# Splitting a mixer's weights two units ahead of the products, in three pairs of buffers

## The chip, the cores and the metric

The kernel runs on one core of one Trainium2 chip. The metric is the device time of one execution in microseconds. The engines are named as in the profile: PE (TensorE matmuls), PEld (TensorE weight loads), DVE (VectorE), ACT (ScalarE), POOL (GpSimd) and SP (SyncE, which here issues nearly all transfers).

## The reference, cut to what matters

Two models run one after the other on 256 tokens of width 1024. The first block has two layers of attention and a convolutional feed-forward network. The second block puts 16 learned tokens in front (L = 272) and has two layers:

```python
for l in range(DEPTH):
    u = rms_norm(h, norm1_g[l])
    p = jnp.einsum("bld,dp->blp", u, w_in[l])
    p_a, p_b, p_c = _split(p, (A_TOTAL, B_TOTAL, C_TOTAL))
    y_a = rwkv7_group(p_a, ...)           # two scan directions, 4 heads
    y_b = diff_attention_group(p_b, ...)
    y_c = gla_group(p_c, ...)             # two scan directions
    h = h + jnp.einsum("blc,cd->bld", concat(y_a, y_b, y_c), w_out[l])
    h = h + expert_choice_ffn(rms_norm(h, norm2_g[l]), router[l], e_w1[l], e_w3[l], e_w2[l])
```

Everything up to the residual sum of `w_out` is called the mixer here; the change touches the two mixers alone. The experts (16 per layer, 1024 by 1408, three matrices each) follow every mixer.

## The kernel before, in words

**Split products.** Where a product needs more than the fast matmul format keeps, both operands are split into a rounded high part and a residual. `split` (L401, L403) makes the high part `whi` of a weight tile of 128 x 1024 with one ACT copy, and the residual `wlo` = weight - `whi` with one subtraction on DVE (on POOL for the 5th and 14th split of a mixer). A product then is three matmuls: high x high, high x residual of the activations, residual x high of the weights. So the third matmul of a unit is the first that needs `wlo`.

**Units.** A mixer has 28 units of projection (a weight tile of up to 128 columns against all 272 tokens: 8 x 3 matmuls) and 8 units of output projection. `units` is a generator: when the program asks for the next unit, it first loads and splits weights until `ahead` units beyond the one handed out are split. The pairs `whi`, `wlo` come from the pool `hl2` with `HL2` pairs; a split must wait until the last matmul that read its pair has ended. The raw weights are loaded by SP into a ring of three tiles (pool `wh`, L1327), and a slot is free when its split is done.

**Order.** PE's order is the program's order (a manual schedule). The program weaves generators: `first` and `second` are the recurrent heads (preparation, then the chains of small products, L1640 to L1824), two more do the other groups, and `others`, the units, fills in between them. The chains wait for named units. In a chain the products of AR and KB (of the first direction, two groups of ten, then of the second) come early; AR and KB are written by DVE at L1566 to L1569. The order on ACT, DVE, POOL and SP is made by the framework's scheduler from the program's order, the priorities and what each instruction waits for. Each of these queues runs in order.

**Memory.** A reserved scratch lies at the low end of each partition. Pools are stacked above it: what lives throughout, then for a mixer its results (`mt`), the ring of weights (`wh`), the normalized activations (`mxu`), the pairs (`hl2`), and above them small working pools, constants, the heads' tiles and the chains' tiles. From the high end hang the first chain's tiles, then the eight output weights, and after the mixer six of the experts' seven large weight buffers. The seventh and three smaller ones are stacked on `mt` from below. A load into an expert buffer waits until all tiles of the mixer that lay there are done with. Of the large ones the first two in use lie 32 to 64 KB below the high end, over the second chain's tiles; the next two lie below these.

The change names `SCR` (L246), `HL2` (L273) and the call of `units` in `project` (L1386 to L1388).

Of the kernel before, what the change touches and what calls it, by code (L numbers as in the profile page):

```python
# [242 lines left out]
EXTRAR = 6  # L243
EXTRAL = 3
EXTRAU = 0
SCR = 16384  # L246
TURN2 = 0
AH = 2
RW = 'tile'
# [20 lines left out]
EXTRA1 = 4  # L270
EXTRA2 = 7
HL1 = 3
HL2 = 2  # L273
TUNE = [{'pool': [5, 14], 'lat': [1.6, 1.846, 1.296, 1.183], 'late': [0, 0, 4.19, 0], 'share': [0.419, 0.319], 'order': [('s', 6), ('s', 7), ('s', 3), ('s', 5), ('s', 1), ('s', 2), ('s', 0), ('gq', 0), ('gk', 0), ('s', 4), ('s', 8), ('gad', 0), ('q', 0), ('q', 1), ('q', 2), ('k', 1), ('k', 2), ('k', 3), ('gv', 0), ('q', 3), ('k', 0), ('gv', 1), ('v', 0), ('v', 1), ('v', 2), ('v', 3), ('sg', 0), ('sg', 1)], 'prep': 2.18, 'last': 2, 'halves': 2.02, 'passes': [0, 2, 1, 3]}, {'pool': [5, 14], 'lat': [1.6, 1.846, 1.296, 1.183], 'late': [0, 0, 4.19, 0], 'share': [0.419, 0.319], 'order': [('s', 6), ('s', 7), ('s', 3), ('s', 5), ('s', 1), ('s', 2), ('s', 0), ('gq', 0), ('gk', 0), ('s', 4), ('s', 8), ('gad', 0), ('q', 0), ('q', 1), ('q', 2), ('k', 1), ('k', 2), ('k', 3), ('gv', 0), ('q', 3), ('k', 0), ('gv', 1), ('v', 0), ('v', 1), ('v', 2), ('v', 3), ('sg', 0), ('sg', 1)], 'prep': 2.18, 'last': 2, 'halves': 2.02, 'passes': [0, 2, 1, 3]}]

# [936 lines left out]
def second_block(K, tap, st=None):  # L1212
# [3 lines left out]
    with ExitStack() as c2x:  # L1216
# [95 lines left out]
        def mixer(l, mixT, swr, cm, ce, nst):  # L1312
# [5 lines left out]
            uT = [U.tile([128, KD, L], F32R, name=f"u{i}") for i in range(2)]  # L1318
            K.hl = cm.enter_context(tc.tile_pool(reuse_waits=RW, name="hl2", bufs=HL2))
            DF = cm.enter_context(tc.tile_pool(reuse_waits=RW, name="df", bufs=1))  # L1320
# [39 lines left out]
            def project(R, box):  # L1360
# [23 lines left out]
                for hp in range(2):  # L1384
                    shifted_to.update({hp: rT[:, hp, :L], 2 + hp: kT[:, hp, :L], 4 + hp: vT[:, hp, :L]})
                us = K.units([unit(JOBS.index(j)) for j in tune["order"]] +  # L1386
                             [lambda i=i, j=j: wouts[2 * i + j][:, None, :] for i in tune["passes"] for j in range(2)],
                             ahead=1)  # L1388

                def cds(name):  # L1390
                    o, n = CD[name]
# [691 lines left out]
            c1, c0 = ExitStack(), ExitStack()  # L2083
            R1 = c1.enter_context(tc.tile_pool(reuse_waits=RW, name="rw1", bufs=1, side="right"))
            prep, rest, us = project(c0.enter_context(tc.tile_pool(reuse_waits=RW, name="mxs", bufs=1)), box)

            def first():
# [376 lines left out]
```

## Time and profile before

| | |
|---|---|
| median of 3 runs | 2652.69 us |
| the three runs | 2651.7, 2652.69, 2666.6 us |
| the profiled execution | 2655.46 us, span 2653.7 us |
| mean granted TensorE clock | 0.948 |
| PE busy | 2462.8 us, 93% |
| PEld busy | 1509.8 us, 57% |
| DVE busy | 1084.4 us, 41% |
| ACT busy | 755.6 us, 28% |
| POOL busy | 207.0 us, 8% |
| read from HBM | 749.54 MB, 283 GB/s over the span |

The span is from the first to the last instruction of the program; an execution takes 1.8 us more. All numbers of a row of the trace belong to one execution, which was 2.8 us above the median. A granted clock of 1.00 is 2.4 GHz and 0.50 is 1.2 GHz; a mean between them is a share of time at either level. A busy share is a mean over stages: the mixers of the second block lie at 769 to 1057 and 1705 to 2003 us, its experts behind them.

### The profile page before, as it was taken

The numbers are of one execution on the slowest core, as the hardware profiler recorded it, in microseconds if no ns is written. First come the engines' busy times: TensorE is split into PE (matmuls) and PEld (weight loads), VectorE is DVE, ScalarE is ACT, GpSimd is POOL, SyncE is SP. The second block draws the span as 40 slices with busy tenths as digits, with TensorE's granted clock in tenths as the row PEclk, the third lists the DMA queues.
The fourth block names the chain that finished last, engine by engine and source line by source line (L and its number), as shares of the span: only waits on it lengthen the run. The fifth ranks groups of instructions, "written<-read, shape, count | busy, mean of one in ns | idle before, by whom it ended". The sixth has DMA issues, their size and how long they took to land. (4 is left out here: it accounts for less than half of the span.)

```text
span 2653.7 us, 43625 instructions
## 1 busy us (share of the span) xinstructions
PE 2462.8 (93%) x18599; PEld 1509.8 (57%) x18599; DVE 1084.4 (41%) x2308; ACT 755.6 (28%) x1471; POOL 207.0 (8%) x260
## 2 busy tenths in 40 slices
PE   6989999899989998999999989999999999899898
PEld 4769988679978876333323322478774333233232
DVE  3557765567668466121111111365563122112112
ACT  3545545545445242110100100253331101000001
POOL 0011011110023211000000000122110000000000
PEclk8999999999989898999999999878899999999999
DMA  9385443674132225999999999511249999999996
GB/s 368 143 367 226 175 168 127 252 307 181 40 109 68 89 89 237 369 426 426 424 426 425 425 425 425 222 59 58 105 168 373 424 426 424 424 426 424 426 425 256
DMA packets 78482, 753.43 MB, mean 284 GB/s; under 512 B 9632, under 2 KB 13616, under 8 KB 25040
## 3 DMA queue, kind: packets, MB, share of 16 engines
q1 hardware_dynamic: 75360, 748.38, 69.2%
q8 instruction: 146, 2.39, 0.4%
q10 hardware_dynamic: 2928, 2.26, 0.3%
q14 instruction: 48, 0.39, 0.0%
HBM read 749.54 MB, written 1.07 MB: 283 GB/s over the span
## 5 line engine op out<-in xcount | busy, mean ns | idle before, releaser
L388 PE MATMUL bank<-w,mixT 128*34 128x512 f32 (+1 forms) x3072 | 685.7, 580 | 77.7 <-DMA w<-in_ew 77.7
L388 PEld LDWEIGHTS bank<-w,mixT 128*34 128x34 f32 x3072 | 190.7, 115 | 539.6 <-issue 401.2
L403 DVE TENSOR_TENSOR wlo<-w,whi 128x1024 fp32r<-128x1024 f32 (+1 forms) x242 | 298.8, 1237 | 169.9 <-ACT whi L401 168.7
L401 ACT ACTIVATE whi<-w 128x1024 fp32r<-128x1024 f32 x246 | 258.2, 1053 | 317.8 <-PE bank L388 131.2
L388 PE MATMUL bank<-w,hT 128*34 128x512 f32 x1408 | 314.6, 594 | 0.0
L2322 ACT ACTIVATE hid<-bank 34x512 f32<-34x512 f32 (+1 forms) x96 | 53.3, 555 | 765.8 <-PE bank L388 765.8
L388 PE MATMUL up<-hF,whi 128*128 128x256 f32 x1408 | 256.5, 285 | 5.2 <-ACT hF L573 5.2
L388 PEld LDWEIGHTS up<-hF,whi 128*128 128x128 f32 x1408 | 219.4, 191 | 6.9 <-ACT hF L573 6.0
L2323 DVE COPY hid<-bank 34x512 f32<-34x512 f32 (+1 forms) x96 | 62.4, 650 | 382.7 <-ACT hid L2322 381.7
L2369 DVE TENSOR_TENSOR x<-x,bank 128x272 f32<-128x272 f32 x256 | 95.7, 433 | 298.1 <-PE bank L388 297.0
L388 PE MATMUL bank<-u,whi 128*128 128x272 f32 (+1 forms) x896 | 212.2, 330 | 2.5 <-ACT u L1293 2.3
L388 PE MATMUL up<-hF,wlo 128*128 128x256 f32 x704 | 199.2, 284 | 0.0
L388 PEld LDWEIGHTS bank<-w,hT 128*34 128x34 f32 x1408 | 77.8, 112 | 189.2 <-issue 187.3
L388 PEld LDWEIGHTS bank<-u,whi 128*128 128x128 f32 (+1 forms) x896 | 151.9, 204 | 20.4 <-issue 7.9
L388 PE MATMUL bank<-u,wlo 128*128 128x272 f32 (+1 forms) x448 | 138.2, 309 | 6.0 <-DVE wlo L403 5.5
L388 PEld LDWEIGHTS up<-hF,wlo 128*128 128x128 f32 x704 | 134.2, 191 | 0.2
L452 POOL TENSOR_TENSOR rr<-rv,ca 128x3 f32<-128x3 f32 (+4 forms) x28 | 32.7, 1170 | 970.6 <-DVE rv L450 966.2
L2360 DVE COPY ys<-bank 34x512 f32<-34x512 f32 x32 | 22.2, 695 | 196.7 <-ACT ys L2359 196.7
L388 PE MATMUL acc<-gh,wlo 128*128 128x256 f32 x352 | 99.1, 281 | 0.0
L388 PE MATMUL acc<-gh,whi 128*128 128x256 f32 x352 | 99.0, 281 | 0.0
L388 PE MATMUL acc<-gl,whi 128*128 128x256 f32 x352 | 99.0, 281 | 0.0
L388 PEld LDWEIGHTS bank<-u,wlo 128*128 128x128 f32 (+1 forms) x448 | 91.6, 204 | 8.1 <-DVE wlo L403 7.0
(501 smaller groups left out, 3409.3 us busy)
## 6 DMA issues: line engine op xcount, KB each, us to landing
w<-in_ew SPq DMA_DIRECT2D x136, 2048.0 KB, 28.3
w<-in_ew SPq DMA_DIRECT2D x94, 1536.0 KB, 27.1
w<-in_ew SPq DMA_DIRECT2D x112, 1024.0 KB, 28.6
w<-in_ada SPq DMA_DIRECT2D x24, 2048.0 KB, 8.3
w<-in_ffn_up SPq DMA_DIRECT2D x22, 2048.0 KB, 8.4
w<-in_w_in SPq DMA_DIRECT2D x54, 512.0 KB, 3.4
w<-in_ffn_down SPq DMA_DIRECT2D x10, 2048.0 KB, 8.3
w<-in_ab_in SPq DMA_DIRECT2D x5, 2048.0 KB, 15.6
```

What stands on the lines that cost most here:

```text
L388: self.nc.tensor.matmul(out, lhsT, rhs, start=start, stop=stop, skip_group_check=True)
L401: self.nc.scalar.activation(v(hi[:, :n]), src, AF.Copy)
L403: (self.nc.gpsimd if self.splits in self.pool_share else self.nc.vector).tensor_tensor(v(lo[:, :n]), src, v(hi[:, :n].bitcast(F32)), op=OP ...
L452: nc.gpsimd.tensor_tensor(r[:, :n], v[:, :n], self.cst("half")[:, :n], op=OP.pow)
L2322: nc.scalar.activation(hb[0:CAP, :n], pu[0:CAP, :n], AF.Copy)
L2323: nc.vector.tensor_copy(hb[64:64 + CAP, :n], pu[64:64 + CAP, :n])
L2360: nc.vector.tensor_copy(ys[64:64 + CAP], py[64:64 + CAP])
L2369: nc.vector.tensor_tensor(x[:, k], x[:, k], pc[:, :L], op=OP.add)
```

## The change

The mixers of the second block split their weights two units ahead of the products in place of one. The pool of split weights gets a third pair of buffers (8 KB per partition). The reserved scratch at the low end shrinks from 16 KB to 1 KB per partition. Nothing else is edited. The index of each split, and so which two run on POOL, is unchanged.

```diff
-SCR = 16384
+SCR = 1024
...
-HL2 = 2
+HL2 = 3
...
                 us = K.units([unit(JOBS.index(j)) for j in tune["order"]] +
                              [lambda i=i, j=j: wouts[2 * i + j][:, None, :] for i in tune["passes"] for j in range(2)],
-                             ahead=1)
+                             ahead=2)
```

## Rows read from the trace of the kernel before

**Rows 1.** The page, part 2: the span in 40 slices of 66 us.

```profile
PEclk8999999999989898999999999878899999999999
DMA  9385443674132225999999999511249999999996
```

**Rows 2.** Table of stretches: from:to, us, busy (instructions) of each engine, granted clock, DMA, GB/s.

```profile
769.00:1057.00 288.00, 266.73 (x3577) 225.71 (x3577) 182.41 (x431) 122.24 (x279) 59.27 (x73) 0.91 0.31 114
1705.00:2003.00 298.00, 276.53 (x3578) 233.73 (x3578) 183.66 (x433) 124.02 (x280) 58.61 (x73) 0.88 0.30 110
...
2003.00:2654.00 651.00, 602.29 (x2953) 211.13 (x2953) 122.49 (x292) 65.30 (x154) 0.85 (x1) 0.96 0.96 402
```

**Rows 3.** Waits of PE in the first mixer: who, for what, us, times, longest.

```profile
PE bank L388 <- DVE wlo L403: 2.2, 2, 1.6
```

**Rows 4.** Waits of PE in the second mixer.

```profile
PE bank L388 <- DVE wlo L403: 3.3, 3, 2.0
```

**Rows 5.** Timeline of PE, second mixer: start, us, instruction, count, [idle before <- releaser].

```profile
1736.90 0.39 PE L388 MATMUL bank<-u,wlo 128*128 128x272 f32 x1 [0.73 <-DVE wlo L403]
...
1739.69 0.42 PE L388 MATMUL bank<-u,whi 128*128 128x272 f32 x2
...
1740.54 1.38 PE L388 MATMUL bank<-AR,KB 64*128 64x128 f32 x10
...
1744.33 0.39 PE L388 MATMUL bank<-u,wlo 128*128 128x272 f32 x1 [1.96 <-DVE wlo L403]
...
1748.17 0.66 PE L388 MATMUL bank<-u,whi 128*128 128x272 f32 x2
```

**Rows 6.** Timeline of DVE, second mixer.

```profile
1740.04 1.02 DVE L1276 COPY bcw<-rr 128x384 f32<-128x384 f32 x1 [1.03 <-POOL rr L1488]
...
1743.06 1.21 DVE L403 TENSOR_TENSOR wlo<-w,whi 128x1024 fp32r<-128x1024 f32 x1
...
1747.07 0.48 DVE L1569 TENSOR_TENSOR KB<-s,s 128x320 f32<-128x320 f32 x1
```

**Rows 7.** Timeline of PE, first mixer.

```profile
801.95 0.39 PE L388 MATMUL bank<-u,wlo 128*128 128x272 f32 x1 [1.58 <-DVE wlo L403]
...
807.10 1.38 PE L388 MATMUL bank<-AR,KB 64*128 64x128 f32 x10
...
812.57 1.38 PE L388 MATMUL bank<-AR,KB 64*128 64x128 f32 x10
```

**Rows 8.** Timeline of DVE, first mixer.

```profile
767.20 0.16 DVE L450 TENSOR_SCALAR rv<-bank 128x3 f32<-128x3 f32 x1 [3.26 <-PE bank L388]
...
810.74 0.49 DVE L1569 TENSOR_TENSOR KB<-s,s 128x320 f32<-128x320 f32 x1
```

**Rows 9.** Timeline of ACT, second mixer.

```profile
1711.99 1.06 ACT L401 ACTIVATE whi<-w 128x1024 fp32r<-128x1024 f32 x1 [1.35 <-PE bank L388]
...
1715.01 1.06 ACT L401 ACTIVATE whi<-w 128x1024 fp32r<-128x1024 f32 x1 [1.58 <-PE bank L388]
...
1736.95 1.05 ACT L401 ACTIVATE whi<-w 128x1024 fp32r<-128x1024 f32 x1
```

**Rows 10.** Table of stretches: seven units in each mixer, and the half-clock stretch.

```profile
799.96:854.01 54.05, 50.44 (x816) 43.06 (x815) 44.26 (x89) 33.69 (x75) 17.54 (x24) 0.97 0.24 72
1735.76:1802.55 66.79, 63.37 (x817) 53.57 (x815) 45.62 (x92) 35.14 (x77) 17.04 (x24) 0.74 0.19 59
...
1745.20:1779.32 34.12, 34.12 (x145) 28.50 (x145) 19.49 (x41) 14.20 (x35) 6.58 (x13) 0.50 0.11 35
```

**Rows 11.** The page, part 6: transfers, count, KB each, median us to landing.

```profile
w<-in_w_in SPq DMA_DIRECT2D x54, 512.0 KB, 3.4
```

**Rows 12.** Waits of SP's queue from 1930 to 2030.

```profile
SPq L378 <- DVE mixT L1824: 41.8, 1, 41.8
```

**Rows 13.** Instructions on the expert weights, 1930 to 2030: count, ns, first and last start.

```profile
L388 PEld LDWEIGHTS bank<-w,mixT x90: 107/112/112, 2010.8 to 2030.0; 128*34 128x34 f32 x90
...
L378 SPq DMA_DIRECT2D w<-in_ew x17: 327/382/737, 1936.9 to 2024.8; - x17
```

**Rows 14.** Table of stretches: the start of the second expert stage.

```profile
2000.00:2014.00 14.00, 11.49 (x67) 8.52 (x69) 5.64 (x20) 1.28 (x4) 0.23 (x1) 0.76 0.71 303
...
2060.00:2620.00 560.00, 520.79 (x2553) 179.72 (x2554) 101.86 (x238) 52.53 (x125) 0.00 (x0) 0.97 1.01 425
```

## The prediction

> **What bounds the kernel now.** I first read the slices of the page [rows 1]. The program alternates: a first block, then twice a mixer followed by 16 experts. In the expert stages DMA is at nine tenths and more without a break. The second view is a table of stretches that I cut at the first product of a mixer and at its routing [rows 2]: the mixers take 288 and 298 us, in which DMA is at 0.31 and 0.30 while PE is busy for 267 and 277 us; the second expert stage has DMA at 0.96. So the change, which touches only the mixers, can act in two ways: by the time at which a mixer ends, and by the time at which the experts' weights may start to come in.
>
> Third, who waited for whom on PE in each mixer [rows 3, 4]. Only the waits for the residuals of the split weights (wlo) concern this change: 2.2 us in two waits in the first mixer and 3.3 us in three in the second, together 5.5 us.
>
> Fourth, the stretch with the longest of these waits, on PE and on DVE [rows 5, 6], and the same program stretch in the other mixer [rows 7, 8]. The reader is to see that in the second mixer PE stands 1.96 us for a wlo that DVE starts only at 1743.06, though its high part had begun on ACT at 1736.95 [rows 9]: DVE had a scan and copies ahead of it. After that wait a pair of the same products takes 0.66 us in place of 0.42 us [rows 5]: the clock has gone from 2.4 to 1.2 GHz, and a table of stretches [rows 10] shows it at 0.50 for 34.1 us. In the first mixer a wait of 1.58 us ends at 801.95. From the start of the unit with that wait (in the second mixer the unit with the wait of 0.73 us) to the start of the unit seven later, the two mixers issue 816 and 817 products and take 54.05 and 66.79 us at a clock of 0.97 and 0.74 [rows 10]: 12.7 us more for the same work.
>
> **The change part by part.** *The split two units ahead.* No instruction is added or removed: the splits (ACT 1.06 us, DVE 1.2 us [rows 6, 9]) are as many as before. PE's order is written by the program and contains no split, so it stays. In steady state a split waits for its pair of buffers, and so starts when PE ends a unit: ACT was released by PE at 1711.99 and 1715.01 [rows 9]. With two pairs the freed pair serves the next unit, with three the one after it. So splits run at the moments at which they run now, and each is ready one unit earlier, at least the 3.0 us between these two ACT rows. The weight loads run three slots ahead and land in 3.4 us [rows 11]; their slots are freed by the same splits, so they keep their places on SP's queue and wait for nothing new. Queued behind a split on ACT and DVE is the chain of the two recurrent heads; as the splits keep their moments, it is held up as much as now. The waits of 2.2 and 3.3 us go, as none is longer than 1.96 us.
>
> *Where the stall goes.* In the first mixer the products of the second direction (AR, KB) come 5.47 us after those of the first (807.10 to 812.57), and the KB that they need is complete at 811.23, 1.34 us earlier [rows 7, 8]. PE and the inputs of DVE's chain (the key norms, sent off right after the wait that ends at 801.95) both move up by 2.2 us, so I count all of it. In the second mixer PE would reach these products at 1740.54 + 5.47 = 1746.0, and 1.3 us earlier still without the two shorter waits before (3.3 - 1.96): 1744.7. DVE works without a hole from 1740.04 until KB is written at 1747.55 [rows 6]; if all of that moves up by 1.3 us, KB is there at 1746.25. So PE would wait 1.5 us for KB where it now waits 1.96 us for wlo: DVE's queue is late next. Of the 3.3 us, 1.8 are left. The bounds are 0.6 (the split of the next unit, 1.21 us, still stands ahead of KB and its forerunner as well) and 3.3 (no split stands there).
>
> *The third split at the start.* It stands in front of the first unit rather than behind it. By the tile sizes of the code the third pair lies where the first block keeps its last squares, so in the first mixer the residuals of units 1 and 2 can be written only after about 764. Two of them (2.4 us) fit into DVE's hole of 3.26 us before 767.20 [rows 8]. I take 0; the bounds are 0 and 1.2 us in each mixer (one residual ahead of the norm's first operation). Below zero is excluded, as nothing waits for that split.
>
> *Memory.* The scratch gives back 15 KB at the low end and the third pair takes 8 KB, so what lies above the pairs starts 7 KB lower, while the first buffers of the expert weights hang from the high end: they overlap less with the mixer's tiles. SP stands 41.8 us for the mixer's last head before it can issue the first expert weights [rows 12], at 1936.9 [rows 13]; those behind them may now come sooner. It is worth nothing: PE uses the first of them at 2010.8 [rows 13], and DMA runs at 0.71 just before, at 1.01 from 2060 on [rows 14]. What ends the stage is the stream that starts when PE frees the first buffer, and this follows the mixer's end. I take 0. The bounds are -4 us (what DMA leaves unused in the stretch before 2014: 0.29 x 14 us) and + 5 us (one weight of 2 MB late, at the 425 GB/s of the last row). The scratch itself serves nothing here: all transfers are issued by SP and ACT.
>
> *The clock.* The half-clock stretch of 34.1 us begins 0.9 us after the longest wait for a split ends, and costs 12.7 us against the other mixer. Whether it goes with the wait is the open question. For it: the first mixer runs the same interleaved stretch at 0.97. Against it: a wait for KB of 1.5 us comes in the same place. I take it to stay.
>
> The Trainium skill (TensorE: Matmul & The Clock Gate, Part 1) says that the low clock is the default state and that activity of the engine releases it. By that rule the clock would have come back by itself soon after 1745, and no 12.7 us would hang on the stall; the sum would be the same as with the stretch kept. The row of that stretch disagrees: PE is busy for 34.12 of 34.12 us there and stays at half [rows 10].
>
> **The sum.** The profiled execution took 2655.46 us: 2653.7 of span and 1.8 around it. The median of the three runs is 2652.69, 2.8 lower, and the lowest 2651.7: they lie so close that I take the long half-clock stretch to be in each. From the median: -2.2 (first mixer) -1.8 (second) = 2648.7; what the shorter waits give back in clock is unknown and small, so I say 2648.
>
> **The rivals.** (a) *The long half-clock stretch goes too.* 2648.7 - 12.7 = 2636, and down to 2652.7 - 5.5 - 12.7 = 2634.5 if no wait for KB appears, less 2 for falls of the clock after the other waits: 2632. It decides whether PE's wait near 1745 falls well under 1.5 us. (b) *Slower: the same stretch appears in the first mixer.* There DVE is only 1.34 us ahead of PE at the second direction's products. If the early residuals, or a split ahead of the scan, put DVE back by more than 1.34 us, PE waits there amid the interleaved products, and the clock falls and stays: + 12.7 - 4 + 1, about 2662. That steps of this size happen fits the third run, 2666.6, 13.9 us above the median. (c) *It doesn't do what it says:* DVE's queue and not the buffer makes the residual late, so it comes as late for its unit as now, and the waits stay: 2652.7. For it: DVE came to the residual of 1743.06 five us after its high part was complete (1736.95 + 1.05). Against: one unit more is longer than any of the waits. (d) *The expert stream starts earlier or later* because of the new places: 2644 to 2653.
>
> **How the numbers follow.** Forecast with the stretch kept 0.43, (a) 0.35, (b) 0.10, (c) 0.07, (d) 0.05. The range 2632 to 2656 takes in all but (b) and some strays. About 1%, 26.5 us, is what a measurement of this kernel can tell from no change: under 2626 none of the cases comes, and over 2679 only two extra stretches would. Faster 0.05, same 0.91, slower 0.04.
>
> **What would show it.** Right: the waits on wlo are gone from PE's list in both mixers, each residual ends a unit earlier against its products, and a wait for KB (or none) stands where 1.96 us stood. (a) shows as a clock near 1.00 where 0.50 stands for 34 us; (b) as such a stretch in the first mixer after its first AR, KB products; (c) as unchanged waits on wlo. The forecast is wrong if ACT's or DVE's order changes so much that steps of the chain are waited for elsewhere, or if SP's first expert loads move behind PE's first use.

## The result, and the profile after

The changed kernel takes 2670.07 us (median of 17 runs), the kernel before 2653.67 us (17 runs beside them): a ratio of 1.0054, 95% interval 1.0042 to 1.0066 (the ratios given here are not those of the medians and differ a little from them). Forecast was 2648 us with a range of 2632 to 2656. So the change costs some 14 to 16 us where a gain of 4.7 was expected.

In the execution that was profiled after the change the clock was at 0.16 from 2625 us on (its own time is 2785.31 us); that end is left out below, and everything is read ahead of it.

The table of stretches answers to [rows 2, 10]. Columns: from:to, length, busy us (instructions) of PE, PE's weight loads, DVE, ACT, POOL; then granted clock, DMA share, GB/s. The first two lines are the seven units of each mixer that stood in [rows 10], the next two the half-clock stretches inside them, the last one the end of the first expert stage.

```profile
804.95:867.73 62.78, 60.11 (x817) 50.94 (x815) 44.62 (x89) 34.15 (x75) 18.12 (x24) 0.78 0.21 62
1749.52:1810.71 61.19, 58.37 (x817) 49.44 (x815) 45.02 (x92) 35.05 (x77) 17.07 (x24) 0.80 0.21 64
817.00:844.31 27.31, 27.31 (x119) 22.52 (x118) 15.00 (x32) 12.72 (x34) 6.07 (x11) 0.50 0.13 39
1762.49:1786.38 23.89, 23.89 (x105) 19.36 (x105) 12.39 (x24) 10.78 (x29) 5.79 (x9) 0.50 0.21 67
...
1684.00:1714.00 30.00, 26.62 (x126) 9.07 (x124) 6.68 (x17) 7.71 (x16) 0.85 (x1) 1.00 0.60 239
```

The first mixer's seven units took 54.05 us at a clock of 0.97 and now take 62.78 us at 0.78; the second mixer's fall from 66.79 to 61.19 us. There is a long half-clock stretch in each mixer now, where only the second had one.

What PE waits for in the first mixer answers to [rows 3] (us in total, times, longest):

```profile
PE bank L388 <- DVE u L1294: 2.0, 2, 1.6
PE bank L388 <- DVE KB L1569: 1.9, 1, 1.9
...
PE bank L388 <- DVE wlo L403: 1.1, 1, 1.1
```

The second mixer's list has the same entries (wlo 1.1 us, KB 2.1 us) in the place of [rows 4]. The waits for wlo of 1.6 and 2.0 us are gone. The 1.1 us that is left is a new one, and the timeline of PE shows where: in the first unit of the mixer (start, us, instruction, count, [idle before <- releaser]).

```profile
770.18 1.30 PE L388 MATMUL bank<-u,whi 128*128 128x272 f32 x2 [1.16 <-ACT u L1293]
772.59 0.59 PE L388 MATMUL bank<-u,wlo 128*128 128x272 f32 x1 [1.11 <-DVE wlo L403]
...
779.45 0.60 PE L388 MATMUL bank<-u,whi 128*128 128x272 f32 x1 [1.61 <-DVE u L1294]
...
787.74 0.42 PE L388 MATMUL bank<-u,whi 128*128 128x272 f32 x2
...
814.00 0.29 PE L388 MATMUL bank<-u,wlo 128*128 128x272 f32 x1
816.19 1.73 PE L388 MATMUL bank<-AR,KB 64*128 64x128 f32 x10 [1.90 <-DVE KB L1569]
817.85 0.82 PE L388 MATMUL bank<-u,whi 128*128 128x272 f32 x2
```

The fourth unit starts at 787.74, 17.56 us after the first; before, the same two starts were 770.12 and 782.16, 12.04 us apart. In the second mixer the distance grew from 11.62 (1706.34 to 1717.96) to 17.57 us (1714.75 to 1732.32). So each mixer loses 5.5 to 6 us at its start. In the first mixer 3.45 us of this are PE's stops after 770.18 (1.11 and 1.61 us as shown, 0.37 and 0.36 us between them); the rest goes mostly with the clock, which comes to its upper level later, too: a pair of these products takes 0.66 us up to 782.1 (before: up to 775.0), then 0.42 us. Further down, PE comes to the second direction's products and waits 1.90 us for KB; behind that wait a pair of products takes 0.82 us, and the clock is at half.

DVE shows the cause of the loss at the start. The same engine of the kernel before is given first (its residuals of the first two units, ahead of the norm), then the changed kernel.

```profile
755.90 1.23 DVE L403 TENSOR_TENSOR wlo<-w,whi 128x1024 fp32r<-128x1024 f32 x1
...
757.12 1.23 DVE L403 TENSOR_TENSOR wlo<-w,whi 128x1024 fp32r<-128x1024 f32 x1
```

```profile
767.26 0.16 DVE L450 TENSOR_SCALAR rv<-bank 128x3 f32<-128x3 f32 x1 [3.41 <-PE bank L388]
769.17 1.31 DVE L1292 SCALAR_TENSOR_TENSOR mixT<-x,v,bank 128x272 f32<-128x272 f32 x3 [1.75 <-PE bank L440]
770.40 0.43 DVE L1294 TENSOR_TENSOR u<-mixT,u 128x272 fp32r<-128x272 f32 x1
770.75 1.78 DVE L403 TENSOR_TENSOR wlo<-w,whi 128x1024 fp32r<-128x1024 f32 x1
...
774.39 1.79 DVE L403 TENSOR_TENSOR wlo<-w,whi 128x1024 fp32r<-128x1024 f32 x1
...
777.27 1.21 DVE L403 TENSOR_TENSOR wlo<-w,whi 128x1024 fp32r<-128x1024 f32 x1
778.41 0.99 DVE L1294 TENSOR_TENSOR u<-mixT,u 128x272 fp32r<-128x272 f32 x1
...
806.86 1.21 DVE L403 TENSOR_TENSOR wlo<-w,whi 128x1024 fp32r<-128x1024 f32 x1
808.00 0.81 DVE L1541 TENSOR_TENSOR_SCAN s<-c,s 128x320 f32<-128x320 f32 x1
809.96 1.02 DVE L1276 COPY bcw<-rr 128x384 f32<-128x384 f32 x1 [1.16 <-POOL rr L1488]
...
812.06 0.67 DVE L1640 TENSOR_TENSOR SK<-bank,c 128x512 f32<-128x512 f32 x1
...
814.15 0.68 DVE L1640 TENSOR_TENSOR SK<-bank,c 128x512 f32<-128x512 f32 x1
...
815.55 0.48 DVE L1569 TENSOR_TENSOR KB<-s,s 128x320 f32<-128x320 f32 x1
```

Not one residual, the upper bound of the prediction, has moved into the norm, but three: they stand between the norm's operations (mixT, u), and the last u, for which PE waits 1.61 us, ends at 779.40. The hole of 3.26 us before the norm [rows 8], in which two of them were to go, is still there, 3.41 us long and empty. It could not take them, as ACT makes the high parts later, too. The first of them in the kernel before, then the first two in the changed kernel:

```profile
754.82 1.05 ACT L401 ACTIVATE whi<-w 128x1024 fp32r<-128x1024 f32 x1
```

```profile
766.24 1.99 ACT L401 ACTIVATE whi<-w 128x1024 fp32r<-128x1024 f32 x2
```

And it is DVE's order that puts the residuals behind mixT and u: from 767.4 DVE stands idle for 1.75 us until it can do mixT, although one high part is complete at about 767.2.

### The profile page after: what moved, and what is told of

Same layout as the page of the kernel before. It is cut to its first block, busy times and chain, and to the rows that moved or that the text cites. A ratio compares the mean times of both kernels' runs of the same rounds, so it can differ in the third digit from the quotient of the medians.

```text
span 2783.6 us, 43632 instructions
## 1 busy us (share of the span) xinstructions
PE 2587.2 (93%) x18599; PEld 1540.3 (55%) x18599; DVE 1086.0 (39%) x2308; ACT 756.8 (27%) x1471; POOL 207.5 (7%) x260
## 5 line engine op out<-in xcount | busy, mean ns | idle before, releaser
L388 PE MATMUL bank<-w,mixT 128*34 128x512 f32 (+1 forms) x3072 | 708.4, 596 | 79.4 <-DMA w<-in_ew 79.4
L388 PE MATMUL bank<-w,hT 128*34 128x512 f32 x1408 | 363.1, 668 | 0.0
L388 PE MATMUL bank<-u,whi 128*128 128x272 f32 (+1 forms) x896 | 217.8, 336 | 7.0 <-DVE u L1294 3.9
L388 PE MATMUL bank<-hT,whi 128*128 128x256 f32 (+1 forms) x464 | 89.4, 295 | 7.7 <-ACT hT L573 3.1
```

The source lines that it names most:

```text
L388: self.nc.tensor.matmul(out, lhsT, rhs, start=start, stop=stop, skip_group_check=True)
```

## Experiments

Each is compared with runs of the kernel before on the same chip, and medians of different groups differ by a few us. The first four form a group (before: 2660.6 us).

**Memory alone.** The edit to the kernel before:

```
-SCR = 16384
+SCR = 1024
```

> The scratch of 1 KB alone: two pairs of buffers, splits one unit ahead. Every engine's order of instructions is that of before; all buffers lie 15 KB lower, except those that hang from the high end. Theory A (the third pair, by its place over the first block's last squares, moves the first three splits into the norm, and costs 5.6 and 5.9 us at the starts of the two mixers): the memory shift alone does nothing, 2650 to 2657 us, first products of the second unit as early as before. Rival B (the loss comes from the new places of all buffers, through the expert stream or the clock): 2664 to 2672 us.

Measured: 2657.46 us, ratio 0.9989 [0.9970, 1.0008]. No difference in time: the new places of all other buffers cost nothing that these runs can tell. Rival B is out.

The profiled execution of this kernel (2651.41 us) shows something else. The long half-clock stretch of the second mixer is not in it, though DVE's order around the wait is that of the kernel before. Here the clock is at half for 3.4 us just ahead of that place, PE comes to the residual later, and waits 0.23 us for it in place of 1.96. The second mixer's wait, and its seven units:

```profile
1749.26 0.39 PE L388 MATMUL bank<-u,wlo 128*128 128x272 f32 x1 [0.23 <-DVE wlo L403]
```

```profile
1740.91:1794.17 53.26, 50.81 (x817) 43.04 (x815) 46.01 (x92) 34.66 (x77) 17.24 (x24) 0.97 0.25 74
```

So the stretch need not come with this order of instructions.

**The third pair alone.** To that, `HL2 = 3`, with `ahead=1` kept.

> Three pairs and the scratch of 1 KB, but splits asked for one unit ahead as before. Theory A (place of the third pair): the first splits again lie inside the norm; the second unit starts some 4.7 us and the third some 5.6 to 5.9 us late in both mixers, and the waits on residuals in steady state stay or go only in part: 2662 to 2672 us. Rival C (the early request of the third split is what costs at the start): the start is as before, 2650 to 2657 us.

Measured: 2673.2 us, 1.0047 [1.0030, 1.0064]. The whole loss is there without the second unit of lead, and so are the two stops for KB (1.9 and 2.1 us). DVE has the three residuals inside the norm again (771.50, 775.13, 778.02); the first and the last:

```profile
771.50 1.78 DVE L403 TENSOR_TENSOR wlo<-w,whi 128x1024 fp32r<-128x1024 f32 x1
...
778.02 1.21 DVE L403 TENSOR_TENSOR wlo<-w,whi 128x1024 fp32r<-128x1024 f32 x1
```

**The lead alone.** The kernel before with one line changed, in two pairs:

```
-                             ahead=1)
+                             ahead=2)
```

> Splits asked for two units ahead, with two pairs and the scratch of 16 KB as before. Theory A (place of the third pair): the first two splits stay ahead of the norm, the third waits for the first unit's buffers as before; no loss at the start, and as a freed pair still serves the next unit but one at the earliest, the waits on residuals stay too: 2648 to 2660 us, the width being what a moved half-clock stretch can do. Rival C (the early request costs at the start): the first residuals inside the norm, 5 to 6 us late in each mixer, 2663 to 2670 us.

Measured: 2643.53 us, 0.9940 [0.9921, 0.9960]: less than both kernels. The start is as before. The waits in steady state did not stay, as expected, but changed their place. PE's waits in the second mixer:

```profile
PE bank L388 <- ACT sqh L1481: 2.9, 2, 2.6
...
PE bank L388 <- DVE wlo L403: 0.2, 1, 0.2
```

PE now stops for sqh, a step earlier, and no long half-clock stretch follows: the second mixer's seven units take 54.12 us at 0.97 in place of 66.79 at 0.74, the first mixer's 53.53 in place of 54.05. So in this profile what the edit gains is the clock; PE's waits for wlo and ACT's sqh together are hardly shorter (second mixer 3.1 us, before 3.5).

**The third pair elsewhere.** The change, with the third pair at the high end of memory, where by the tile sizes neither the first block's squares nor the last expert's tiles lie:

```
-K.hl = cm.enter_context(tc.tile_pool(reuse_waits=RW, name="hl2", bufs=HL2))
+two = cm.enter_context(tc.tile_pool(reuse_waits=RW, name="hl2", bufs=2))
+third = cm.enter_context(tc.tile_pool(reuse_waits=RW, name="hl3", bufs=1, side="right"))
+K.hl = Turn(two, two, third)
```

(`Turn` gives each unit's two tiles from the next of its pools in turn.)

> The change as made, but the third pair is taken from the high end of memory, where nothing of the first block or of the last expert lies; the first two pairs lie where they lay, 15 KB lower. Theory A (place of the third pair): the first splits are ahead of the norm again, so the 5.6 and 5.9 us at the starts come back, the waits of 1.58 and 1.96 us stay away: 2670 - 11.5 = 2658 us if the half-clock stretch in the first mixer stays, 2645 us if it goes as well. Rival C (the early request itself costs at the start): 2668 to 2672 us, the third split's residual holding the norm up.

Measured: 2649.42 us, 0.9963 [0.9949, 0.9977]. DVE has the first residuals ahead of the norm again (compare 755.90 and 757.12 above):

```profile
756.47 1.23 DVE L403 TENSOR_TENSOR wlo<-w,whi 128x1024 fp32r<-128x1024 f32 x1
...
757.69 1.22 DVE L403 TENSOR_TENSOR wlo<-w,whi 128x1024 fp32r<-128x1024 f32 x1
```

The fourth unit starts 12.08 and 11.65 us after the first in the two mixers, as in the kernel before. Theory A holds for the start: the place of the third pair, and nothing else in the change, puts the first splits into the norm. (The time falls between its two figures, 2658 and 2645 us.) The stretches of this kernel, the seven units of each mixer:

```profile
800.00:851.46 51.46, 48.30 (x816) 41.44 (x814) 45.15 (x89) 33.53 (x75) 18.13 (x24) 1.00 0.26 76
1727.00:1789.71 62.71, 60.06 (x817) 50.93 (x815) 45.08 (x92) 35.17 (x77) 17.05 (x24) 0.78 0.21 63
```

A stop of 1.92 us for KB in the first mixer cost no clock here, one of 2.11 us in the second did.

The next four ask about the clock. They form a second group (before: 2657.73 us).

> The changed kernel once more, on the same chip as the next three, for a profile whose end is undisturbed. All theories: 2666 to 2673 us, a wait for KB of 1.9 and 2.1 us on PE ahead of the second direction's products of the two mixers, a half-clock stretch of 24 to 27 us behind each of them (theory D below), or behind only one of them in some runs (rival E).

Measured: 2675.84 us, 1.0070 [1.0047, 1.0092]; both stops (1.90 and 2.09 us) and both stretches (23.9 us each) are there.

**PE kept at work.** In the changed kernel, ahead of the second direction's first products, into the bank that they clear:

```
+[K.mm(b4[:, :L], uT[0][:, 0, 0:128], uT[0][:, 0]) for _ in range(16 * (d == 1 and hh == 0 and hp == 1))]
```

> The change, and in each mixer 16 extra products of 272 columns, whose results nothing reads, ahead of the second direction's first AR, KB products, so that PE works while it would wait for KB. Theory D (the two half-clock stretches begin because PE stands still for 1.9 and 2.1 us): the stretches of 27 and 24 us go, the extra products cost nothing as KB is no earlier: 2670 - 13 - 11 = 2646 us. Rival E (the clock falls there by itself, by what PE executes in the interleaved stretch): the stretches stay, 2668 to 2674 us.

Measured: 2649.39 us, 0.9972 [0.9955, 0.9989], 26.5 us less than without the extra products. PE's timeline and the seven units of each mixer:

```profile
814.43 2.19 PE L388 MATMUL bank<-u 128*128 128x272 f32 x16
816.55 1.38 PE L388 MATMUL bank<-AR,KB 64*128 64x128 f32 x10
```

```profile
805.26:856.84 51.58, 50.50 (x833) 43.53 (x831) 45.17 (x89) 33.50 (x75) 18.14 (x24) 1.00 0.26 76
1742.76:1794.31 51.55, 50.75 (x832) 43.64 (x830) 46.12 (x92) 34.49 (x77) 17.30 (x24) 1.00 0.27 76
```

KB's products start as late as in the changed kernel (816.55), but the clock stays at 1.00 to the end of the seven units. The same in the kernel with the third pair at the high end:

> The change with the third pair at the high end, and the same 16 extra products. Theory D: the one stretch of 27 us that the kernel with the third pair at the high end showed in its second mixer goes: 2649 - 12 = 2637 us, and runs near 2659 are gone. Rival E: 2647 to 2651 us, with the stretch in place.

Measured: 2638.37 us, 0.9938 [0.9918, 0.9958]; the clock is at 1.00 in the seven units of both mixers.

And in the kernel before, at the start of the ninth unit (`pad` such products in `unit3` for that unit alone), where PE waits 1.96 us for a residual in the second mixer (the wait of 1.58 us in the first lies a unit earlier, other than the text below has it, and stayed, so that there the extra products cover no wait and cost 2 us: seven units take 56.04 us for 54.05):

> The kernel before, and 16 extra products of 272 columns, whose results nothing reads, at the start of the ninth unit of each mixer, ahead of the wait of 1.58 and 1.96 us for that unit's residual. Theory D: the half-clock stretch of 34 us in the second mixer does not begin: 2654 - 13 = 2641 us (2 to 3 us more if the extra products reach past the end of the wait). Rival E: 2652 to 2660 us, the stretch in place.

Measured: 2644.43 us, 0.9962 [0.9944, 0.9980]. The second mixer's seven units:

```profile
1735.17:1788.22 53.05, 50.98 (x832) 43.48 (x831) 45.59 (x92) 34.43 (x77) 16.85 (x24) 1.00 0.26 74
```

Theory D holds in all three: 2649, 2638 and 2644 us measured for 2646, 2637 and 2641 expected.

The last four, in two groups (before: 2657.28 and 2658.73 us), go at what is left. First the kernel with the third pair at the high end, with `ahead=1`.

> Three pairs with the third at the high end, splits asked for one unit ahead only. Theory F (with three pairs it is the third pair that takes the waits for residuals away, and the second unit of lead adds nothing, as ACT and DVE have the splits in nearly the same place in their order either way): 2646 to 2652 us as with two units of lead, no waits for wlo, one or two half-clock stretches behind waits for KB. Rival G (the lead is needed): the waits of 1.58 and 1.96 us for wlo are back, 2652 to 2658 us.

Measured: 2651.27 us, 0.9982 [0.9966, 0.9999]; no waits for wlo, the same stops for KB (1.93 and 2.11 us). Theory F: with a third pair the lead adds nothing that these runs can tell apart.

Then half as many extra products (8 for 16 in the line above).

> The third pair at the high end, two units of lead, and 8 extra products instead of 16 ahead of the second direction's first AR, KB products: PE works for 0.9 of the 2 us and stands still for 1.1. Theory D, if a stop of about 1 us at this place is short enough (stops of 1.1 us for a split and of 0.96 us for sqh were not followed by long stretches in the kernels so far): 2637 to 2641 us, no long stretch. If any stop at this place suffices: 2647 to 2651 us with a stretch of 24 to 27 us in the second mixer.

Measured: 2640.39 us, 0.9935 [0.9916, 0.9954]. PE stands still for 0.82 us (1.00 in the second mixer), and the seven units stay at full clock:

```profile
808.88 1.18 PE L388 MATMUL bank<-u 128*128 128x272 f32 x8
810.88 1.38 PE L388 MATMUL bank<-AR,KB 64*128 64x128 f32 x10 [0.82 <-DVE KB L1569]
```

Last, two tries to have KB earlier, by giving a residual to GpSimd (`'pool': [5, 9, 14]` and `[5, 10, 14]` in place of `[5, 14]`).

> The third pair at the high end, and the ninth residual of each mixer on GpSimd (2.4 us there) in place of VectorE (1.21 us), where it stood ahead of the second direction's scan. Theory H (the wait for KB is VectorE's queue: two residuals ahead of the scan, products' copies ahead of KB): KB comes 1 us or more earlier against PE, the waits of 1.9 and 2.1 us shrink to about 1 or go, no long half-clock stretch: 2636 to 2642 us. Rival I (the wait hangs on GpSimd's 2.9 us for the key norm's power, behind which the residual now stands): the waits stay or grow by up to 2.4 us, 2647 to 2655 us.

> As the kernel before, but the tenth residual goes to GpSimd, where it stands directly ahead of the key norm's power. Theory H: one residual less ahead of the scan and the copies of the first direction's products behind KB: the waits for KB shrink to about 1 us or go, 2636 to 2642 us. Rival I: the power comes up to 2.4 us later, so do the copy that spreads it and KB behind it on VectorE: waits of 1.9 us and more stay, 2647 to 2655 us.

Measured: 2652.43 us, 0.9980 [0.9959, 1.0000], and 2664.7 us, 1.0028 [1.0011, 1.0045]. Neither gained time, and the second lies above what either theory gave. With the ninth residual on GpSimd the first mixer has no stop for KB any more, but one of 1.21 us for sqh a step earlier, and no long stretch; the second mixer's stop grew to 2.92 us. With the tenth the stops grew to 2.85 and 4.15 us, and both mixers had a long stretch. Rows of the kernel with the tenth, on DVE and on POOL:

```profile
802.53 2.56 DVE L1541 TENSOR_TENSOR_SCAN s<-c,s 128x320 f32<-128x320 f32 x1 [0.30 <-issue]
```

```profile
801.82 2.58 POOL L403 TENSOR_TENSOR wlo<-w,whi 128x1024 fp32r<-128x1024 f32 x1 [1.01 <-ACT whi L401]
804.37 1.84 POOL L1488 TENSOR_TENSOR rr<-rv,ca 128x6 f32<-128x6 f32 x1
```

The power (rr) starts only when GpSimd has done the residual, as rival I has it, and the scan, 0.81 us elsewhere, takes 2.56 us beside it. So KB's lateness has to do with GpSimd as well as with DVE's queue; what would make it earlier stays open.

## Why the prediction was wrong

The medians of the second group split the loss, each term the difference of two kernels:

- the two stops for KB and their half-clock stretches, after the change: 2675.84 - 2649.39 = 26.5 us
- the third pair's place, both mixers together: 2649.39 - 2638.37 = 11.0 us
- what the change gains when neither kernel has a long stretch at these places: 2638.37 - 2644.43 = -6.1 us, of which 2 us are the extra products that cover no wait in the first mixer of the kernel before
- the one stop and stretch that the kernel before had: 2644.43 - 2657.73 = -13.3 us

Together +18.1 us, which is the difference of 2675.84 and 2657.73 by construction; what the runs add is the size of each. The sizes are rough: each kernel's interval is some 5 us either way, and by the ratios the terms are about 26, 9, -6 and -10 us. The first is far outside this; the second is borne out by the traces; the gain of 6 us alone could not be told from none.

**What bounds the kernel: right.** In the kernel with the third pair at the high end and 16 extra products, the second expert stage's first product comes 19.9 us earlier than in the kernel before (1990.96 for 2010.83) and the span is 20.1 us shorter (2633.6 for 2653.7). What a mixer gains or loses arrives at the end.

**The waits for residuals: right that they go.** Those of 1.6 and 2.0 us are gone. The prediction did not part the lead from the pair. The runs do: the third pair removes the waits with a lead of one, and the lead with two pairs turns them into stops for sqh.

**"The third split at the start": the step that failed.** It was taken as 0, with 1.2 us per mixer as its upper bound. It costs 5.5 and 6 us in the trace and 11.0 us in the runs. The prediction had seen that the third pair lies where the first block keeps its last squares, and that two residuals would have to wait for about 764. What failed is the overlap that it then counted on: that these two fit into DVE's hole before 767.20 and delay nothing. That takes their high parts to be ready and the splits to run as soon as their buffers are free. In the changed kernel the splits of all three units come later in ACT's and DVE's order. The high parts of the first two, which began at 754.8 and 756.0, begin at 766.2 and about 767.2, directly behind ACT's copy of the norm's sums, and three residuals of 1.2 to 1.8 us land among the norm's operations. Why all three splits moved in the order, and not only those whose buffers lie over the squares, no run shows. The second mixer loses as much, where the prediction had looked at no tile under the pair at all; with the pair at the high end both losses are gone.

**"Where the stall goes": mis-sized.** In the first mixer no wait for KB was expected, in the second 1.5 us; it is 1.9 and 2.1. The inputs did move up with PE, but KB did not move up with its inputs. PE has nothing else to do 9.3 us after the start of the unit with the former wait, in place of 12.6 us: 3.3 us earlier. GpSimd's power, on which KB hangs, is there 2.8 us earlier against the same start (the copy behind it begins at 809.96 for a start of 804.95). The same copy in the kernel before, for a start of 799.96:

```profile
807.78 0.36 DVE L1276 COPY bcw<-rr 128x384 f32<-128x384 f32 x1 [2.06 <-POOL rr L1488]
```

Yet KB is complete 11.08 us after that start (804.95 to 816.03), before 11.27 us (799.96 to 811.23 [rows 8, 10]). From that copy to KB DVE takes 6.07 us in place of 3.45: In the kernel before it had done part of that work before the power came, and then stood idle for 2.06 us. Now the copy itself takes 1.02 us for 0.36, another copy (bm) now stands behind it and no longer ahead, and three operations on the first direction's products (SK) come in between where there was one. That these came up in the order because PE issues those products earlier is likely, but no run shows it.

**The clock: rival (b) came true, and was held for unlikely (0.10).** Its outcome was named rightly: PE waits for KB amid the interleaved products, and the clock falls and stays. Its cause was not: DVE was not put back, its KB is 0.2 us earlier against the unit's start, and the 1.34 us of lead went because PE came 3.3 us earlier. Its time, 2662 us, lacks the loss at the start. The second mixer's stretch stayed, as forecast, though shorter (23.9 us for 34.1).

The Trainium skill (TensorE: Matmul & The Clock Gate, Part 1) has the engine's activity release the low clock. The stretch of 27.31 us, in which PE is busy for 27.31 us at 0.50, disagrees once more. What the runs with extra products agree with is the other half of that section, that standing idle is what brings the low clock; the stretch behind a stop of 0.59 us, shown at the end, fits that less well.

**Memory and the expert stream: right** at nothing, as far as the first experiment can tell (0.9970 to 1.0008).

**"They lie so close that I take the long half-clock stretch to be in each": too quick.** The runs of before spread over 25 us (2641.06 to 2666.6), and with the smaller scratch alone one execution did without the stretch. The end of an expert stage differs as well between executions of one kernel: in the last line of the first table 126 products take 30 us at 1.00. When the changed kernel ran again, at the same place:

```profile
1684.00:1720.00 36.00, 32.76 (x128) 11.21 (x126) 7.53 (x19) 7.80 (x17) 0.85 (x1) 0.79 0.49 187
```

So between single profiles some 5 us at such a place mean nothing.

## What to carry to other kernels

A buffer that is added costs what lies under it: look at which instructions must now come behind the last use of that memory, count all that share their queue with the new one, and try another place before giving the buffer up. When a wait is removed, ask what each of the two sides hangs on: here the waiting engine moved up by 3 us against the unit's start and the work it needed next did not, so that the wait came back with another name. And a stop of 2 us in dense products can cost several times its length in clock (10 to 13 us for one of 1.96, 26 us for two); a few products that nobody reads, put where the engine would stand still anyway, gave that back.

## What the runs showed of the hardware

**A stop of about 2 us and the long half-clock stretch.** The stops for KB ahead of the second direction's products, with the half-clock stretch behind each: 1.90 and 2.11 us (27.3 and 23.9 us), 1.90 and 2.09 (23.9 and 23.9), 1.90 and 2.08 (23.9 and 27.3), 2.11, 2.11 and 2.92 (27.3 each), 2.85 (23.9), 4.15 (30.7). Two of 1.92 and 1.93 us, in the first mixer with the third pair at the high end, were followed by none, nor were those of 0.82 and 1.00. In the six mixers of the kernels with 16 extra products there is no such stretch at this place. Why 1.90 and 1.92 us differ is open, and so is why a stop of 2.65 us for sqh in the kernel with the lead alone had no long stretch behind it. All the long ones, and that of 34.1 us in the kernel before, end shortly before PE comes to the 80 products of 32x32 (T, SK), at most 1.8 us ahead of the first of them. In the second mixer with the third pair at the high end the stretch ends at 1766.34:

```profile
1766.15 0.51 PE L388 MATMUL bank<-u,whi 128*128 128x272 f32 x2
...
1766.72 0.89 PE L388 MATMUL bank<-T,SK 32*32 32x32 f32 x80
```

The length of a stop does not settle it. Later in each mixer, also of the kernels with 16 extra products, the clock falls twice more. Around the stop for dk (1.9 to 2.2 us) it is at half for 6.8 to 13.7 us only. And in the recurrent chain it is at half for 6.8 to 17.1 us, behind a stop that can be as short as 0.59 us, here in the kernel with the third pair at the high end and 16 extra products:

```profile
862.81 0.81 PE L388 MATMUL bank<-T,SK 32*32 32x32 f32 x20 [0.59 <-DVE Wm L1721]
```

```profile
863.50:881.00 17.50, 16.92 (x134) 14.42 (x131) 4.80 (x9) 4.89 (x11) 1.52 (x2) 0.51 0.12 37
```

So that a stop of 1 us costs no clock holds for the place where it was tried, and no rule for other places follows from these runs.

**VectorE stands still beside GpSimd.** With the ninth residual on GpSimd (798.11 to 800.73, first mixer), a DVE operation of 0.35 us elsewhere took 2.46:

```profile
798.42 2.46 DVE L1479 TENSOR_SCALAR kk<-kT,v 128x272 f32<-128x272 f32 x1
```

It ends about when GpSimd's instruction does (800.88 and 800.73). The Trainium skill (SBUF — State Buffer, Who interferes with whom) says that GpSimd shares its pair of ports with VectorE's second pair, and that the one that issues first holds it for the whole instruction while the other, if it needs it, is blocked; the trace agrees, though it does not show which ports an instruction used. The same shows in the residuals inside the norm: 1.78 and 1.79 us beside GpSimd's u (0.84 us, from 770.62), 1.2 us alone.

The hold-up goes the other way, too. In the first mixer of the changed kernel GpSimd's power for KB takes 2.91 us beside DVE's residual and scan (806.86 to 808.81). In the kernel before it took 1.33 us (from 806.42), with DVE idle for most of it.

```profile
807.02 2.91 POOL L1488 TENSOR_TENSOR rr<-rv,ca 128x6 f32<-128x6 f32 x1 [1.50 <-DVE rv L1486]
```

DVE then waits 1.16 us for it, so this is part of the first mixer's stop for KB. In the second mixer the power takes 1.32 us, and the stop is 2.11 us all the same.
